# Attention 0: the rotation's cosine product of heads 1 to 7, from the matmul's bank on VectorE instead of from ScalarE's copy on GpSimd

## The chip, the cores and the metric

The kernel runs on one core of a Trainium2 chip. The metric is the device time of one execution in microseconds, and a kernel's time is the median of its runs. A core's engines work side by side and each takes its instructions in order: TensorE (PE in the profile, its weight loads PEld), VectorE (DVE), ScalarE (ACT), GpSimd (POOL) and SyncE (SP), whose queue issues the DMAs. Matmul results land in banks of PSUM, which VectorE and ScalarE read; GpSimd works on SBUF.

## What is computed

Two layers over 1024 tokens of width 1024, float32. Layer 0 is differential attention, and the change lies in it:

```python
q = _rope(q.reshape(b, s, 2 * DA_HEADS, DA_QK_DIM), positions)
k = _rope(k.reshape(b, s, 2 * DA_HEADS, DA_QK_DIM), positions)
...
sc = jnp.einsum('bqhcd,bkhcd->bhcqk', qb, k, preferred_element_type=f32) * scale
p = jax.nn.softmax(sc, axis=-1)
p = p[:, :, 0] - lam * p[:, :, 1]
return jnp.einsum('bhqk,bkhd->bqhd', p.astype(v.dtype), v)
```

with 8 heads of two 64-wide parts each, and the rotation

```python
x1, x2 = xf[..., :half], xf[..., half:]
out = jnp.concatenate([x1 * cos - x2 * sin, x2 * cos + x1 * sin], axis=-1)
```

A normalization over each head's output, a SiLU gate and an output projection follow; layer 1 is latent attention (MLA), which has a rotation of its own that the change does not touch.

## The kernel before

Matmul operands are split into a high and a low part in float32r, and each product is three matmuls (L173 to L175). Projections are made transposed: a strip of 128 weight columns against 512 tokens (a half) gives a bank of 128 x 512 (`acc`); a head of layer 0 has a k, a q and a z strip of two halves each. Attention 0 goes head by head. For each tile of 128 queries (`q_tile`) TensorE makes two scores of 128 x 1024 (`s`, L866), VectorE takes the negated maximum (`nm`, L412), ScalarE the exponential (L414, `e`, and in place in `s`), VectorE combines the two (L872 to L874, `e`). TensorE transposes that in two halves (`tr`, L395), ScalarE copies the high part (`pth`, L397), VectorE subtracts the low part (`ptl`, L398), and TensorE multiplies by the values (`pv`). Between these pieces TensorE makes the strips of the next head, some steps at a time (`stream0`, the table `FILL0`): so the rotation of head 1's strips runs from 157 us on, and that of head 7's to about 628 us.

When a half of a k or q strip is done, `rope` takes its bank: ScalarE copies it to SBUF (`rp_raw`, L331, or L333 with the scale for q), four DMAs on SP's queue swap its blocks of 32 partitions into `rp_sw` (L335), and `rp_r` gets the product with the cosines (L336). Some steps of the stream later, GpSimd makes the product of the swapped tile with the sines (L341) and the sum (L343). Then ScalarE and GpSimd split the result for the scores: for k in `stack_k` (L356 to L359, `ks`), for q in `stack_q` (ScalarE L364 and L365, `qa`; GpSimd L366 and L367, `qb`; then four DMAs on SP's queue, L369 and L370). In heads 1 to 7 the product and the sum are GpSimd's; in head 0 VectorE makes both. 7 heads x k and q x 2 halves make 28 rotations.

GpSimd also makes the low parts of the weights (`wl`, L219), the gate (`o`, L938), the scaling by the head's norm (L908), products for the output projection (`ob`, L1112 to L1123) and the power in the norm (`rq_y`, L169). The norm's sums come from eight matmuls (`ssq`, L945) that use a bank of the same rotation as the strips, and VectorE turns them into `sl_w` and `sl_f` (L949 to L951) for GpSimd's L169.

The order of each engine's instructions is made by the framework's scheduler from the program's order and its own costs; `in_turn` keeps an instruction in the program's order on its engine (nearly all of GpSimd's), `behind` puts one behind a mark of the softmax. Buffers are rings by tag: all of `rope`'s tiles come from one of six. Two banks serve `acc` in turn.

Of the kernel before, what the change touches and what calls it, by code (L numbers as in the profile page):

```python
# [16 lines left out]
ALU = mybir.AluOpType  # L17
# [55 lines left out]
SC0 = 64 ** -0.5  # L73
# [8 lines left out]
def trunk(ctx: ExitStack, tc: tile.TileContext, A, out):  # L82
    nc = tc.nc
    SP, PE, V, S, G = nc.sync, nc.tensor, nc.vector, nc.scalar, nc.gpsimd

    def pool(stack, name, bufs=1, side="left", space=None):
        kw = dict(name=name, bufs=bufs, reuse_waits="tile")
        if space is not None:
            kw["space"] = space
            if space == DRAM:  # L90
                kw.pop("reuse_waits")
        else:
            kw["side"] = side
        return stack.enter_context(tc.tile_pool(**kw))
# [21 lines left out]
    def bank(tag, name, shape=None):  # L116
        nonlocal turn
        if tag == "acc":
            turn += 1
            if (turn - 1) % (2 + NB.get("accx", 0)) < 2:  # L120
                return psa.tile([P, HF], F32, name=name, tag="acc", bufs=2)
            tag = "accx"
        return ps.tile(shape or [P, HF], F32, name=name, tag=tag, bufs=NB[tag])
# [20 lines left out]
    cosT = const.tile([P, T], F32, name="cosT")  # L144
# [35 lines left out]
    def behind(eng):  # L180

        return tc.issue_after(mk[eng]) if eng in mk else nullcontext()

    def in_turn(ins):

        return tc.keep_in_program_order(ins) if mk else ins
# [134 lines left out]
                self.count += 1  # L321
                side.tick()

    def rope(rp, acc, half, scale, eng=G, add=V):

        cs = slice(half * HF, half * HF + HF)
        raw = rp.tile([P, HF], F32, name="rp_raw", tag="rp", bufs=6)
        sw = rp.tile([P, HF], F32, name="rp_sw", tag="rp", bufs=6)
        r = rp.tile([P, HF], F32, name="rp_r", tag="rp", bufs=6)
        if scale == 1.0:  # L330
            S.copy(raw, acc)  # L331
        else:
            S.mul(raw, acc, scale)  # L333
        for q in range(4):
            SP.dma_start(sw[q * 32 : q * 32 + 32], raw[(q ^ 1) * 32 : (q ^ 1) * 32 + 32])  # L335
        r_ = eng.tensor_mul(r, raw, cosT[:, cs])  # L336
        if eng is G:
            in_turn(r_)

        def rot():  # L340
            in_turn(G.tensor_mul(sw, sw, sinT[:, cs]))  # L341
            if add is G:
                in_turn(G.tensor_add(r, r, sw))  # L343

        def fin():
            if add is not G:
                with behind("V"):
                    V.tensor_add(r, r, sw)
            return r

        return rot, fin

    def stack_k(t, r):

        with behind("S"):
            S.copy(t[0:64, 0, :], r[0:64])  # L356
            S.copy(t[64:128, 1, :], r[64:128])
        in_turn(G.tensor_sub(t[64:128, 0, :], r[0:64], f32v(t[0:64, 0, :])))
        in_turn(G.tensor_sub(t[0:64, 1, :], r[64:128], f32v(t[64:128, 1, :])))  # L359

    def stack_q(qa, qb, r):

        with behind("S"):
            S.copy(qa[0:64, 0, :], r[0:64])  # L364
            S.copy(qa[64:128, 1, :], r[64:128])  # L365
        in_turn(G.tensor_sub(qb[0:64, 0, :], r[0:64], f32v(qa[0:64, 0, :])))  # L366
        in_turn(G.tensor_sub(qb[64:128, 1, :], r[64:128], f32v(qa[64:128, 1, :])))  # L367
        for t in (qa, qb):
            SP.dma_start(f32v(t[64:128, 0, :]), f32v(t[0:64, 0, :]))  # L369
            SP.dma_start(f32v(t[0:64, 1, :]), f32v(t[64:128, 1, :]))  # L370
# [133 lines left out]
    wp = pool(stW, "wp0", side="right")  # L504
# [262 lines left out]

    def k_done(h):
        def f(acc, half):
            rot, fin = rope(wp, acc, half, 1.0, *[G if h else V] * 2)  # L770

            def g():
                t = a0a.tile([P, 2, HF], F32R, name="ks", tag="ks", bufs=4)
                stack_k(t, r.pop() if r else fin())
                KS.setdefault(h, [None, None])[half] = t

            r = []
            sum_ = [lambda: r.append(fin()), None] if h else []
            side.add(*[None] * ROT, rot, *[None] * (DEF - 1 - ROT), *sum_, g)
        return f  # L780

    def q_done(h):
        def f(acc, half):
            rot, fin = rope(wp, acc, half, SC0, *[G if h else V] * 2)

            def g():
                qa = a0a.tile([P, 2, HF], F32R, name="qa", tag="qs", bufs=4)
                qb = a0a.tile([P, 2, HF], F32R, name="qb", tag="qs", bufs=4)
                stack_q(qa, qb, r.pop() if r else fin())
                QS.setdefault(h, [None, None])[half] = qa, qb  # L790

            r = []
            sum_ = [lambda: r.append(fin()), None] if 0 < h < 5 else []
            side.add(*[None] * ROT, rot, *[None] * (DEF - 1 - ROT - (h == NH - 1)), *sum_, g)
        return f
# [728 lines left out]
    for n, rows, acc, f in ((3, 4, Z, 1), (4, 0, Z, 1), (5, 4, Y, 1), (6, 4, Y, 0)):  # L1524
# [5 lines left out]
        for i in range(4):  # L1530
# [24 lines left out]
            if i == 1 and n == 5:  # L1555
                raws = [[], []]
                with tc.issue_after(w6):
                    for k, (tag, nb) in enumerate((("wraw", 2), ("gz", 3))):
                        for f in range(2):
                            raw = wst.tile([P, HF], F32, name="wraw", tag=tag, bufs=nb)  # L1560
# [27 lines left out]
    wp = pool(stw, "wp1", side="right")  # L1588
# [432 lines left out]
    def qp_done(h):  # L2021
        def f(acc, half):
            rot, fin = rope(wp, acc, half, SC1, G, G if h or half else V)

            def g():
                qa = ap.tile([P, 2, HF], F32R, name="qpa", tag="qps", bufs=4)
                qb = ap.tile([P, 2, HF], F32R, name="qpb", tag="qps", bufs=4)
                stack_q(qa, qb, fin())
                QP.setdefault(h, [None, None])[half] = qa, qb

            side.add(None, rot, *[None] * (h > 0 and not half))
            if h and half:
                late_q.append(g)
            elif half:
                first_q.append(g)
            else:
                side.add(g)
        return f
# [209 lines left out]
    def add_to(tt, acc, f, a=0, b=HF, piece=False):  # L2248
        full = xs_[tt]
        cs = slice(f * HF + a, f * HF + b)  # L2250
        add = V.tensor_add(full[:, cs], full[:, cs], acc[:, a:b])
        if not piece:
            return add.ins
        early = tt // 4
        ss = sm.tile([P, 1], F32, name="tss")
        junk = p6.tile([P, HF], BF16, name="tjunk", tag="tjunk", bufs=1)
        sq = S.activation(junk[:, : b - a], full[:, cs], AF.Square, accum_out=ss).ins
        final = f != early and b == HF
        w = w_[tt] if early else w4[:, tt : tt + 1]
        if f == early:  # L2260
            V.tensor_scalar(w, ss, 1.0 / D, EPS, op0=ALU.mult, op1=ALU.add)
            G.tensor_mul(full[:, cs], full[:, cs], fg[:, cs])
        else:
            sums = V.scalar_tensor_tensor(out=w, in0=ss, scalar=1.0 / D, in1=w, op0=ALU.mult, op1=ALU.add).ins
        if not final:
            return add.ins
        if tt == NT - 1:
            for f_, ins in zip(held, (sums, sq)):
                with tc.issue_after(ins):
                    f_()  # L2270
        if early:
            scale(tt, rsqrt(w, 1)[:, 0:1])
        elif tt == 3:
            y4.append(rsqrt(w4, 4))
# [72 lines left out]
    for n, first, rows, acc, f, piece in ((3, True, 4, Z, 1, False), (4, False, 0, Z, 1, True), (5, False, 4, Y, 1, True)):  # L2347
        sp = sv.splits(n + 1)
        for i in range(4):
# [5 lines left out]
            add = add_to(rows + i, acc[i], f, piece=piece)  # L2355
# [8 lines left out]
    for tiles, a, b in LAST1:  # L2364
        acc = {i: bank("z", "oyb") if a else Y[i] for i in tiles}
# [87 lines left out]
```

## Time and profile before

| | before |
|---|---|
| median of 3 runs, us | 1395.75 (1395.17 to 1396.02) |
| profiled execution, us | 1394.95 |
| its span, us | 1393.2 |
| granted TensorE clock | 0.999 |
| busy us: PE, PEld | 1367.5, 1144.7 |
| busy us: DVE, ACT, POOL | 928.3, 740.9, 753.1 |

The profile is of one execution, and its times are from the span's start. A group's row gives the line, engine, operation, the tile written and those read, count, busy time and mean. A timeline's row gives start, duration, engine, line, operation and tiles, and in square brackets the engine's idle time ahead of it with what ended it. Matmuls are pipelined, so that rows of TensorE overlap. "x36" for L336 in the page counts the eight rotations of layer 1 that are GpSimd's as well.

### The profile page before, as it was taken

To read this page: it belongs to the slowest core of one execution; us is meant where nothing else is said; L and a number is where in the kernel's file an instruction comes from. 1 tells how busy PE (TensorE), PEld (TensorE's weight loads), DVE (VectorE), ACT (ScalarE), POOL (GpSimd) and SP (SyncE) were. 2 spreads that over 40 slices of the span, in tenths; PEclk is the share of its full clock that TensorE was granted. 3 is DMA by queue.
4 is the path that set the end of the run, shared out by engine and by line. 5 is a ranking of instruction groups with operands and counts; after the bars stand their busy time and mean duration, and the time that the engine had idled before them with its cause. 6 is when DMAs were issued, how large, how long until landed. Compare 5 with 4: busy or idle time off the path is not lost.

```text
span 1393.2 us, 20695 instructions
## 1 busy us (share of the span) xinstructions
PE 1367.5 (98%) x7334; PEld 1144.7 (82%) x7334; DVE 928.3 (67%) x1313; ACT 740.9 (53%) x1339; POOL 753.1 (54%) x593
## 2 busy tenths in 40 slices
PE   9999999999999999999999999999999999999997
PEld 6788888888888887887887888888888888888886
DVE  7655777777666666668596976545656555555684
ACT  5532465656565555567648553335454544545554
POOL 5424374758686858575794233532141373834673
PEclk9999999999999999999999999999999999999999
DMA  9857644343444434526564246489443364667463
GB/s 342 263 177 244 201 110 141 100 144 105 149 127 144 128 121 122 151 61 212 182 219 167 68 137 212 137 282 286 125 105 119 102 201 136 193 221 215 145 245 121
DMA packets 149386, 232.06 MB, mean 167 GB/s; under 512 B 20641, under 2 KB 57633, under 8 KB 149282
## 3 DMA queue, kind: packets, MB, share of 16 engines
q1 hardware_dynamic: 149282, 230.74, 52.7%
q8 instruction: 58, 0.95, 0.3%
q14 instruction: 46, 0.38, 0.1%
HBM read 144.74 MB, written 61.81 MB: 148 GB/s over the span
## 4 chain that ended last, share of the span: by engine, by line
PE 79%; DVE 6%; DMA 5%; ACT 3%; POOL 3%; issue 2%; SPq 1%; POOLq 0%; ACTq 0%; DVEq 0%
PE s L2067 10%; PE acc L173 9%; PE acc L175 9%; PE acc L174 9%; PE tr L395 7%; PE s L866 7%; PE pv L173 4%; PE pv L174 4%; PE pv L175 4%; PE vps L173 2%; PE vps L174 1%; PE vps L175 1%; PE zacc L175 1%; PE zacc L173 1%; PE zacc L174 1%
## 5 line engine op out<-in xcount | busy, mean ns | idle before, releaser
L397 ACT CAST pth<-tr 128x512 fp32r<-128x512 f32 x256 | 150.3, 587 | 285.7 <-PE tr L395 280.8
L412 DVE TENSOR_REDUCE nm<-s 128x1 f32<-128x1024 f32 x192 | 233.8, 1218 | 79.8 <-PE s L866 70.9
L398 DVE TENSOR_TENSOR ptl<-tr,pth 128x512 fp32r<-128x512 f32 x256 | 176.1, 688 | 150.3 <-ACT pth L397 146.3
L219 POOL TENSOR_TENSOR wl<-wraw,wh 128x512 fp32r<-128x512 f32 (+2 forms) x77 | 98.8, 1284 | 208.4 <-ACT wh L218 176.3
L414 ACT ACTIVATE e<-s,nm 128x1024 f32<-128x1024 f32 x128 | 143.5, 1121 | 35.4 <-DVE nm L412 35.0
L395 PE MATMUL tr<-ident,e 128*128 128x128 f32 x1024 | 155.0, 273 | 4.1 <-DVE ptl L398 3.8
L395 PEld LDWEIGHTS tr<-ident,e 128*128 128x128 f32 x1024 | 120.7, 140 | 46.5 <-DVE ptl L398 24.1
L173 PE MATMUL acc<-h0h,wh 128*128 128x512 f32 x360 | 150.2, 417 | 0.0
L173 PE MATMUL pv<-pth,vt 128*128 128x256 f32 x512 | 147.5, 288 | 0.0
L174 PE MATMUL pv<-ptl,vt 128*128 128x256 f32 x512 | 145.6, 284 | 0.0
L175 PE MATMUL pv<-pth,vt 128*128 128x256 f32 x512 | 144.6, 282 | 0.0
L175 PE MATMUL acc<-h0h,wl 128*128 128x512 f32 x360 | 141.5, 393 | 0.0
L174 PE MATMUL acc<-h0l,wh 128*128 128x512 f32 x360 | 141.1, 392 | 0.0
L336 POOL TENSOR_TENSOR rp_r<-rp_raw,cosT 128x512 f32<-128x512 f32 x36 | 47.0, 1305 | 104.4 <-ACT rp_raw L333 52.9
L173 PEld LDWEIGHTS pv<-pth,vt 128*128 128x128 f32 x512 | 97.2, 190 | 2.9 <-ACT pth L397 0.2
L174 PEld LDWEIGHTS pv<-ptl,vt 128*128 128x128 f32 x512 | 97.4, 190 | 2.4
L175 PEld LDWEIGHTS pv<-pth,vt 128*128 128x128 f32 x512 | 97.3, 190 | 0.0
L1199 POOL TENSOR_TENSOR wol<-wol,woh 128x512 fp32r<-128x512 f32 x56 | 82.3, 1492 | 26.0 <-ACT woh L1198 24.4
L866 PE MATMUL s<-ks,qa 128*128 128x512 f32 x256 | 82.7, 403 | 4.4 <-DVE e L874 3.2
L874 DVE SCALAR_TENSOR_TENSOR e<-s,z,e 128x1024 f32<-128x1024 f32 x64 | 82.2, 1284 | 2.2
L866 PE MATMUL s<-ks,qb 128*128 128x512 f32 x256 | 79.8, 393 | 1.2 <-DMA qb<-qb 1.2
L175 PEld LDWEIGHTS acc<-h0h,wl 128*128 128x128 f32 x360 | 67.6, 188 | 15.1
(427 smaller groups left out, 3461.1 us busy)
## 6 DMA issues: line engine op xcount, KB each, us to landing
ada<-in_ada_ss SPq DMA_DIRECT2D x32, 512.0 KB, 5.9
wraw<-in_w_s SPq DMA_DIRECT2D x64, 256.0 KB, 2.8
vS<-v_hl SPq DMA_DIRECT2D x32, 512.0 KB, 5.9
vt<-vS SPq DMA_DIRECT2D x32, 512.0 KB, 4.9
wol<-tS SPq DMA_DIRECT2D x56, 256.0 KB, 5.2
tS<-ob SPq DMA_DIRECT2D x48, 256.0 KB, 2.0
rp_sw<-rp_raw SPq DMA_DIRECT2D x160, 64.0 KB, 2.0
bc_s<-bc_d SPq DMA_DIRECT2D x34, 256.0 KB, 4.2
```

The source lines that it names most:

```text
L173: PE.matmul(psum, ah, bh, start=first, stop=False, skip_group_check=skip)
L174: PE.matmul(psum, ah, bl, start=False, stop=False, skip_group_check=skip)
L175: mm3.last = PE.matmul(psum, al, bh, start=False, stop=last, skip_group_check=skip).ins
L219: sub = (V if pair_of else G).tensor_sub(l_[:, :n], raw[:, :n], f32v(h_[:, :n]))
L395: transpose_p.last = PE.transpose(tr[:, j, :], p[:, kt * P : (kt + 1) * P], ident).ins
L397: mk["S"] = S.copy(pth[kh][:, :, dst], tr).ins
L398: mk["V"] = V.tensor_sub(ptl[kh][:, :, dst], tr, f32v(pth[kh][:, :, dst])).ins
L412: mk["V"] = V.reduce_max(nm, s_ps, axis=AX.X, negate=True).ins
L414: mk["S"] = S.activation(e, s_ps, AF.Exp, bias=nm, scale=1.0, accum_out=zs).ins
L866: PE.matmul(s_ps[:, kc * HF : (kc + 1) * HF], src[:, c, ql], KS[h][kc][:, c, :], start=fst, stop=not fst)
L1199: sub = eng.tensor_sub(lo, raw, f32v(hi))
L2067: PE.matmul(s_ps[:, kc * HF : (kc + 1) * HF], lhs, rhs(kc), start=i == 0, stop=i == 4)
```

## The change

`rope` gets a flag, which `k_done` and `q_done` set for heads 1 to 7. With it, VectorE multiplies the bank by the scale and the cosines in one instruction; GpSimd's product of ScalarE's copy is gone from those rotations. The copy and the swap stay.

```diff
-    def rope(rp, acc, half, scale, eng=G, add=V):
+    def rope(rp, acc, half, scale, eng=G, add=V, bank_=False):
...
         for q in range(4):
             SP.dma_start(sw[q * 32 : q * 32 + 32], raw[(q ^ 1) * 32 : (q ^ 1) * 32 + 32])
-        r_ = eng.tensor_mul(r, raw, cosT[:, cs])
-        if eng is G:
-            in_turn(r_)
+        if bank_:
+            V.scalar_tensor_tensor(out=r, in0=acc, scalar=scale, in1=cosT[:, cs], op0=ALU.mult, op1=ALU.mult)
+        else:
+            r_ = eng.tensor_mul(r, raw, cosT[:, cs])
+            if eng is G:
+                in_turn(r_)
...
-            rot, fin = rope(wp, acc, half, 1.0, *[G if h else V] * 2)
+            rot, fin = rope(wp, acc, half, 1.0, *[G if h else V] * 2, h > 0)
...
-            rot, fin = rope(wp, acc, half, SC0, *[G if h else V] * 2)
+            rot, fin = rope(wp, acc, half, SC0, *[G if h else V] * 2, h > 0)
```

The new product is line 337; the lines after it stand three further down in the changed kernel (L398 is L401 there). VectorE is not held to the program's order, so the scheduler places the 28 products. On VectorE at the q strip of head 1 (some 180 us into the span before; `rp_r` is the rotated tile, `z` the softmax's sums, `ada` a product of the modulation), before:

```order
L412 TENSOR_REDUCE nm<-s 128x1 [waits PE_49]
L398 TENSOR_TENSOR ptl<-tr,pth 128x4x128 [waits Activation_49]
L436 ISA ada,modb_105<-ada,c_202,vec 128x1024 [waits DMAHW1_49]
L436 ISA modb_105 128x1
L872 RECIPROCAL z_1670<-z_1670 128x1 [waits Activation_49]
L873 TENSOR_SCALAR z_1670<-z_1670,zz,neglam 128x1 [waits DVE_49]
L874 SCALAR_TENSOR_TENSOR e<-s,z_1670,e 128x1024 [waits DVE_49]
```

and in the changed kernel:

```order
L415 TENSOR_REDUCE nm<-s 128x1 [waits PE_49]
L401 TENSOR_TENSOR ptl<-tr,pth 128x4x128 [waits Activation_49]
L439 ISA ada,modb_105<-ada,c_202,vec 128x1024 [waits DMAHW1_49]
L439 ISA modb_105 128x1
L875 RECIPROCAL z_1670<-z_1670 128x1 [waits Activation_49]
L337 SCALAR_TENSOR_TENSOR rp_r<-acc,cosT 128x512 [waits Activation_49,Pool_49]
L876 TENSOR_SCALAR z_1670<-z_1670,zz,neglam 128x1 [waits DVE_49]
L877 SCALAR_TENSOR_TENSOR e<-s,z_1670,e 128x1024 [waits DVE_49]
```

One instruction came in; it waits for ScalarE, whose copy reads the same bank, and for GpSimd's last use of the buffer that `rp_r` takes over. On GpSimd at the k and q strips of head 5 (460 to 474 us), before:

```order
L1119 TENSOR_TENSOR ot_4671<-ob_4305,ob_4304 128x512 [waits Pool_49]
L336 TENSOR_TENSOR rp_r<-rp_raw,cosT 128x512 [waits Activation_49]
L358 TENSOR_TENSOR ks<-rp_r,ks 64x512 [waits Activation_49,Pool_49]
L359 TENSOR_TENSOR ks<-rp_r,ks 64x512 [waits Activation_49]
L219 TENSOR_TENSOR wl<-wraw,wh 128x512 [waits PE_49,Activation_49,Pool_49]
L938 TENSOR_TENSOR o<-o,gz 128x512 [waits Activation_49]
L1122 TENSOR_TENSOR ob_4304<-ot_4671,ob_4304 128x512
L1123 TENSOR_TENSOR ob_4305<-ob_4305,ot_4671 128x512 [waits DMAHW1_49]
L341 TENSOR_TENSOR rp_sw<-rp_sw,sinT 128x512 [waits DMAHW3_49,DMAHW4_49,DMAHW2_49,DMAHW1_49]
L343 TENSOR_TENSOR rp_r<-rp_r,rp_sw 128x512 [waits Pool_49]
```

and in the changed kernel:

```order
L1122 TENSOR_TENSOR ot_4671<-ob_4305,ob_4304 128x512 [waits Pool_49]
L361 TENSOR_TENSOR ks<-rp_r,ks 64x512 [waits Activation_49,Pool_49]
L362 TENSOR_TENSOR ks<-rp_r,ks 64x512 [waits Activation_49]
L219 TENSOR_TENSOR wl<-wraw,wh 128x512 [waits PE_49,Activation_49,Pool_49]
L941 TENSOR_TENSOR o<-o,gz 128x512 [waits Activation_49]
L1125 TENSOR_TENSOR ob_4304<-ot_4671,ob_4304 128x512
L1126 TENSOR_TENSOR ob_4305<-ob_4305,ot_4671 128x512 [waits DMAHW1_49]
L344 TENSOR_TENSOR rp_sw<-rp_sw,sinT 128x512 [waits DMAHW3_49,DMAHW4_49,DMAHW2_49,DMAHW1_49]
L346 TENSOR_TENSOR rp_r<-rp_r,rp_sw 128x512 [waits DVE_49,Pool_49]
```

The product is gone, the rest stands in the same order, and the sum waits for VectorE. On TensorE at the q strip's neighbourhood of head 4 (365 us), where the sums of the norm are made, before:

```order
L866 MATMUL s<-ks,qb 128x512 x2
L945 MATMUL ssq<-ones,osq 128x1 [waits Activation_49]
L945 MATMUL ssq<-ones,osq 128x1 x3
L173 MATMUL acc<-h0h_1_120,wh 128x512
L174 MATMUL acc<-h0l_1_121,wh 128x512
L175 MATMUL acc<-h0h_1_120,wl 128x512
L395 MATMUL tr<-ident,e 128x128 [waits DVE_49]
```

and in the changed kernel:

```order
L398 MATMUL tr<-ident,e 128x128 [waits DVE_49]
L398 MATMUL tr<-ident,e 128x128 x3
L173 MATMUL acc<-h0h_1_124,wh 128x512
L174 MATMUL acc<-h0l_1_125,wh 128x512
L175 MATMUL acc<-h0h_1_124,wl 128x512
L869 MATMUL s<-ks,qa 128x512 [waits DVE_49]
L948 MATMUL ssq<-ones,osq 128x1 [waits DVE_49]
L948 MATMUL ssq<-ones,osq 128x1 x3
L869 MATMUL s<-ks,qa 128x512
```

Those matmuls moved behind the next transposes and into the next tile's score, and wait for VectorE's product where they waited for ScalarE. They moved so in two heads; in five earlier ones they stay in place and wait for VectorE too. In some tiles TensorE's transposes stand a step of the stream later or earlier than before; the instructions are the same.

## The prediction

> **What bounds the kernel now.** I read the page's busy times and chain first, then busy time by stretch of the span, then TensorE's own waits in order of time, and last what GpSimd, ScalarE and VectorE do ahead of each of those waits.
>
> ```profile
> PE 1367.5 (98%) x7334; PEld 1144.7 (82%) x7334; DVE 928.3 (67%) x1313; ACT 740.9 (53%) x1339; POOL 753.1 (54%) x593
> PE 79%; DVE 6%; DMA 5%; ACT 3%; POOL 3%; issue 2%; SPq 1%; POOLq 0%; ACTq 0%; DVEq 0%
> ```
>
> TensorE is busy for 1367.5 of 1393.2 us and makes 79% of the chain that ended last. No change to VectorE or GpSimd is worth more than the TensorE waits that they cause, so the question is which of these lie where the products are.
>
> ```profile
> 157.00:330.00 173.00, 172.91 (x972) 147.81 (x971) 133.59 (x191) 105.41 (x187) 113.51 (x89) 1.00 0.42 120
> 330.00:400.00 70.00, 69.41 (x389) 58.53 (x387) 49.23 (x70) 41.25 (x74) 50.82 (x43) 1.00 0.44 132
> 400.00:470.00 70.00, 68.54 (x387) 58.16 (x387) 46.85 (x66) 40.34 (x71) 54.92 (x46) 1.00 0.44 136
> 470.00:540.00 70.00, 68.29 (x380) 56.82 (x378) 46.75 (x65) 40.45 (x72) 51.11 (x43) 1.00 0.45 138
> 540.00:640.00 100.00, 98.31 (x553) 82.80 (x552) 69.82 (x99) 59.19 (x104) 67.61 (x56) 1.00 0.39 115
> 640.00:700.00 60.00, 56.12 (x322) 46.31 (x321) 41.59 (x66) 38.49 (x73) 38.98 (x33) 1.00 0.65 211
> ```
>
> The columns are the stretch, its length, then busy time of PE, PEld, DVE, ACT and POOL, TensorE's clock, DMA share and GB/s. From 157 to 640 us, where the 28 products lie, TensorE idles for 0.09 + 0.59 + 1.46 + 1.71 + 1.69 = 5.5 us. GpSimd is busy for 338 of these 483 us (70%), VectorE for 346 (72%). After 640 no product runs. These are TensorE's waits there:
>
> ```profile
> 334.49 0.73 PE L866 MATMUL s<-ks,qa 128*128 128x512 f32 x2 [0.59 <-DVE e L874]
> 409.96 0.70 PE L866 MATMUL s<-ks,qa 128*128 128x512 f32 x2 [0.88 <-DMA qa<-qa]
> 411.22 0.70 PE L866 MATMUL s<-ks,qb 128*128 128x512 f32 x2 [0.55 <-DMA qb<-qb]
> 475.10 0.66 PE L395 MATMUL tr<-ident,e 128*128 128x128 f32 x4 [0.87 <-DVE ptl L398]
> 490.83 0.73 PE L866 MATMUL s<-ks,qa 128*128 128x512 f32 x2 [0.65 <-DVE e L874]
> 543.54 0.73 PE L866 MATMUL s<-ks,qa 128*128 128x512 f32 x2 [0.32 <-DVE e L874]
> 551.32 0.70 PE L866 MATMUL s<-ks,qb 128*128 128x512 f32 x2 [0.66 <-DMA qb<-qb]
> 561.02 0.74 PE L866 MATMUL s<-ks,qa 128*128 128x512 f32 x2 [0.30 <-DVE e L874]
> 615.16 0.66 PE L395 MATMUL tr<-ident,e 128*128 128x128 f32 x4 [0.40 <-DVE ptl L398]
> ```
>
> Nine waits, 5.22 us together. That is all the change can win in this stage. It can lose more, because most of these waits end on VectorE, which gets the work.
>
> **What is removed and added.** The tile of the products, and VectorE's nearest row, a product of a bank and an SBUF tile with the same shape:
>
> ```profile
> L336 POOL TENSOR_TENSOR rp_r<-rp_raw,cosT x28: 1264/1294/1392, 158.1 to 617.7; 128x512 f32<-128x512 f32 x28
> L802 DVE SCALAR_TENSOR_TENSOR gz<-zth,acc x20: 665/684/689, 110.9 to 860.5; 128x512 f32<-128x512 f32 x20
> ```
>
> GpSimd loses 28 x 1.294 = 36.2 us, VectorE gains 28 x 0.684 = 19.2 us. ScalarE's copy of the bank stays, since the four swap DMAs read it; no DMA is added or taken away. Neither sum is a time by itself.
>
> **Where GpSimd's 1.3 us reaches TensorE.** Ahead of the wait at 475.10:
>
> ```profile
> 460.18 1.30 POOL L336 TENSOR_TENSOR rp_r<-rp_raw,cosT 128x512 f32<-128x512 f32 x1
> 470.64 1.29 POOL L343 TENSOR_TENSOR rp_r<-rp_r,rp_sw 128x512 f32<-128x512 f32 x1
> 471.96 0.62 ACT L364 CAST qa<-rp_r 64x512 fp32r<-64x512 f32 x1 [2.23 <-POOL rp_r L343]
> 473.74 0.58 ACT L397 CAST pth<-tr 128x512 fp32r<-128x512 f32 x1
> 474.36 0.69 DVE L398 TENSOR_TENSOR ptl<-tr,pth 128x512 fp32r<-128x512 f32 x1 [0.94 <-ACT pth L397]
> ACT qa L364 <- POOL rp_r L343: 9.5, 6, 2.3
> ```
>
> GpSimd works without a gap from 460 to 472, so the sum L343 is late; ScalarE stands still for 2.23 us behind it, with the next softmax's copy queued after it; VectorE's subtraction follows, and TensorE waits 0.87. Without the product at 460.18 all of this comes 1.3 us earlier, more than 0.87: I take the whole wait. The wait at 490.83 has the same form one half later (the last row: ScalarE waits for L343 9.5 us in all, six times, 2.3 at most), because SP issues that half's swap DMAs behind the qb transfer that GpSimd releases: 0.65, taken whole too. At 334.49 it goes through VectorE itself:
>
> ```profile
> 331.63 1.28 POOL L336 TENSOR_TENSOR rp_r<-rp_raw,cosT 128x512 f32<-128x512 f32 x1
> 331.72 1.22 DVE L951 TENSOR_SCALAR sl_w<-sl_w 128x4 f32<-128x4 f32 x1
> 333.15 1.28 DVE L874 SCALAR_TENSOR_TENSOR e<-s,z,e 128x1024 f32<-128x1024 f32 x1
> L951 DVE TENSOR_SCALAR sl_w<-sl_w x16: 152/170/1221, 196.4 to 689.1; 128x4 f32<-128x4 f32 x16
> ```
>
> A 128x4 instruction with a median of 170 ns takes 1.22 us here and ends when the GpSimd product ends: it stood behind it. The next GpSimd instruction needs its result, so without the product nothing is in its way: 1.05 us earlier against a wait of 0.59, taken whole. At 410:
>
> ```profile
> 404.53 1.28 POOL L336 TENSOR_TENSOR rp_r<-rp_raw,cosT 128x512 f32<-128x512 f32 x1
> 407.14 1.29 POOL L367 TENSOR_TENSOR qb<-rp_r,qa 64x512 fp32r<-64x512 f32 x1
> 409.49 0.52 SPq L370 DMA_DIRECT2D qb<-qb  x1
> ```
>
> GpSimd has two products in the backlog ahead of L367, but SP's queue issues in order and follows by only one of them, 1.3 us. That takes the 0.88 and some 0.2 of the 0.55: 1.1. Of the three waits at 543 to 561 (0.32 + 0.66 + 0.30 = 1.28), which hang on one more late L951 and on a qb transfer, I take half, 0.6, since their swap transfer and the head's output on ScalarE end close by. The one at 615 I leave. Sum: 0.87 + 0.65 + 0.59 + 1.1 + 0.6 = **3.8 us**; ends 0 (every chain has something else just behind) and 5.2 (all nine).
>
> **What VectorE's 0.68 us costs.** In the new order each product waits for ScalarE's copy of the same bank, so it can't start earlier than the GpSimd one did; the built order has it at 28 places. Laying 0.69 us into VectorE's timeline at each, after its predecessor there or the copy, whichever ends last, delays the next VectorE instruction by 11.0 us in all; the rest falls where VectorE stood idle. TensorE pays only where its own instruction stands closer behind. The first and the last of seven such places:
>
> ```profile
> 157.51 1.21 DVE L412 TENSOR_REDUCE nm<-s 128x1 f32<-128x1024 f32 x1
> 159.07 0.69 DVE L398 TENSOR_TENSOR ptl<-tr,pth 128x512 fp32r<-128x512 f32 x1 [0.35 <-ACT pth L397]
> 159.88 0.49 PE L395 MATMUL tr<-ident,e 128*128 128x128 f32 x3
> ...
> 507.80 1.22 DVE L412 TENSOR_REDUCE nm<-s 128x1 f32<-128x1024 f32 x1
> 508.93 0.68 DVE L398 TENSOR_TENSOR ptl<-tr,pth 128x512 fp32r<-128x512 f32 x1
> 510.07 0.38 PE L395 MATMUL tr<-ident,e 128*128 128x128 f32 x2
> ```
>
> At 159 the product fills the idle 0.35 and delays the subtraction by 0.34; the transposes come 0.12 after it, so TensorE loses 0.22. At 509 there is no idle time: 0.77 against a margin of 0.46, a loss of 0.31. The five between read 0.47, 0.47, 0.11, 0.40 and 0.20. Sum **2.2 us**; ends 0 (TensorE's order also moved at such places, transposes later) and 11.0 (no margin anywhere).
>
> The waits it adds: seven of the ssq matmuls, which reuse the bank just finished, now wait for VectorE's product instead of ScalarE's copy. In the timeline the product would end 0.4 us or more ahead of each, and two of them moved 2 to 3 us later in TensorE's order, so I cost this at nothing; the cover is gone if VectorE is over 0.4 us later there. Behind a product that waits, VectorE holds the next softmax's maximum.
>
> Net 2.2 - 3.8 = -1.6 us. The profiled execution took 1394.95 us and goes to about 1393.35; the median of the three runs stands 0.8 above it, so I predict 1395.75 - 1.6 = **1394.1**.
>
> **A rule of the notes.** The Trainium skill, Perfetto Trace Analysis, Optimizing Scalar/DVE Operations, says that GpSimd and VectorE share an SBUF read port, so that moving work between them might not help; SBUF — State Buffer, Who interferes with whom, limits this to VectorE instructions with two SBUF inputs or in a two-port mode. The L951 row agrees with the sharing and the L802 row with the limit; by the first page alone the time would be that of the third rival below.
>
> **Rivals.** *The backlog unwinds.* GpSimd's lateness is a queue, and 11% less work (36 of 338 us) may drain it wholly: all nine waits go, 5.2, and VectorE's cost falls to about 1 with the L951 stretches gone: -4.2, 1391.5. For it: five of the nine have GpSimd in their chain. Against: the margins of TensorE elsewhere are as thin.
>
> *VectorE is held by ScalarE* (slower). Product waits for copy, copy for L364, L364 for GpSimd; now VectorE stands in that line too, with the softmax's maximum behind it. It decides once the copies land more than about 1 us later than in this trace, which uses up the idle time at the places read above: then all of the 11.0 is paid, less the 3.8 won: +7.2, 1403.0. Against: in the timeline the copy has ended when VectorE gets to the product, or ends in idle time there, and GpSimd's relief makes the copies earlier.
>
> *The products contend.* If each stood behind a running GpSimd instruction as L951 did, half of 1.29 us in 70% of cases, 28 x 0.645 x 0.70 = 12.6 us more of VectorE, a fifth of it (2.2 / 11.0) paid by TensorE: +2.5, net +0.9, 1396.7. Against: the spread of L802, 665 to 689 ns, beside a GpSimd that is as busy.
>
> **How the numbers follow.** 0.2% of 1395.75 is 2.8 us, about what a measurement here can tell from no change: faster is below 1392.95, slower above 1398.55. The forecast and the contention, both inside, hold 0.50 (the contention 0.08 of it); the unwound backlog 0.33; VectorE held, and anything like it above 1398.55, 0.17. The range runs from 1390.5, all nine waits gone at no cost (5.2 below), to 1399.5, half of the way to the held VectorE, which leaves about 0.1 on each side.
>
> **What would show it.** Right: 28 products on VectorE at 0.67 to 0.69 us; GpSimd down by 36 us; ScalarE's waits for L343's sum well under 9.5 us; no TensorE wait near 334, 475 and 490; new waits of 0.2 to 0.5 us on the subtraction or the combination in heads 1 to 3. Wrong: products of over 0.8 us, ssq matmuls waiting for VectorE, or TensorE's idle time from 157 to 640 above 5.5 us. The prediction fails most easily if the waits that vanish come back at other tiles.

## The result and the profile after

Three comparisons of the changed kernel with the kernel before were made, each with its own runs of both:

| comparison | before, median us | changed, median us (lowest to highest) | ratio, 95% interval | that is |
|---|---|---|---|---|
| with the prediction | 1396.02 | 1392.52 (1390.75 to 1394.0) | 0.9973 [0.9962, 0.9985] | -3.8 us [-5.3, -2.1] |
| repeated (e5) | 1395.86 | 1394.17 (1391.49 to 1397.15) | 0.9986 [0.9978, 0.9995] | -2.0 us [-3.1, -0.7] |
| repeated (e11) | 1396.21 | 1394.26 (1391.55 to 1395.95) | 0.9985 [0.9976, 0.9994] | -2.1 us [-3.4, -0.8] |

The changed kernel is faster by 2 to 4 us, some 0.2%; the mean of the three is 2.6. The forecast was 1.6, the first rival (the backlog unwinds) 4.2. The first comparison's interval holds the rival's time and leaves out the forecast; in both repeats it is the other way round.

From the page of the changed kernel and its busy time by stretch, columns as before:

```profile
PE 1367.2 (98%) x7334; PEld 1145.0 (82%) x7334; DVE 942.0 (68%) x1341; ACT 741.5 (53%) x1339; POOL 717.9 (52%) x565
```

```profile
157.00:330.00 173.00, 172.42 (x970) 147.54 (x969) 141.67 (x202) 104.52 (x185) 98.61 (x77) 1.00 0.42 122
330.00:400.00 70.00, 70.00 (x394) 59.72 (x393) 49.98 (x74) 42.58 (x76) 47.71 (x40) 1.00 0.44 132
400.00:470.00 70.00, 69.25 (x390) 58.53 (x389) 48.02 (x71) 40.21 (x72) 51.08 (x43) 1.00 0.47 141
470.00:540.00 70.00, 69.13 (x383) 57.65 (x383) 49.22 (x72) 40.77 (x72) 46.26 (x39) 1.00 0.44 138
540.00:640.00 100.00, 99.30 (x563) 83.97 (x563) 73.69 (x110) 60.20 (x106) 60.41 (x51) 1.00 0.39 114
```

GpSimd lost 35.2 us over the span, of 36.2 worked out. VectorE gained 16.3 us in these stretches (346.3 to 362.6), not 19.2. Rows of VectorE that follow one another without a gap overlap by 0.08 us (the product at 507.50 takes 0.68, and the next row starts at 508.10, as shown further down), so that a product between two others adds only 0.60 us of busy time: 28 x 0.60 = 16.8, an estimate. TensorE now idles from 157 to 640 us for 0.58 + 0.00 + 0.75 + 0.87 + 0.70 = 2.9 us, where it was 5.5. These are its waits of over 0.1 us there:

```profile
166.79 0.73 PE L869 MATMUL s<-ks,qa 128*128 128x512 f32 x2 [0.58 <-DVE e L877]
409.40 0.70 PE L869 MATMUL s<-ks,qa 128*128 128x512 f32 x2 [0.19 <-DMA qa<-qa]
410.63 0.70 PE L869 MATMUL s<-ks,qb 128*128 128x512 f32 x2 [0.53 <-DMA qb<-qb]
489.37 0.73 PE L869 MATMUL s<-ks,qa 128*128 128x512 f32 x2 [0.73 <-DVE e L877]
549.33 0.70 PE L869 MATMUL s<-ks,qb 128*128 128x512 f32 x2 [0.43 <-DMA qb<-qb]
558.98 0.73 PE L869 MATMUL s<-ks,qa 128*128 128x512 f32 x2 [0.27 <-DVE e L877]
```

Of the nine waits of before those at 334, 475, 543 and 615 are gone, that at 410 is smaller, those at 411, 490, 551 and 561 are still there, and one at 166.8 is new. The products themselves, and ScalarE's wait for GpSimd's sum, which was 9.5 us in all:

```profile
L337 DVE SCALAR_TENSOR_TENSOR rp_r<-acc,cosT x28: 670/686/693, 159.3 to 614.5; 128x512 f32<-128x512 f32 x28
...
ACT qa L367 <- POOL rp_r L346: 5.5, 6, 1.7
```

**How the profiled execution adds up.** It took 1393.23 us, 1.7 below that of before. VectorE's row maximum `nm` is a good clock inside a trace: its first and its 121st instruction bracket the 28 products. Of before and of after:

```profile
141.84 1.21 DVE L412 TENSOR_REDUCE nm<-s 128x1 f32<-128x1024 f32 x1
...
649.40 1.21 DVE L412 TENSOR_REDUCE nm<-s 128x1 f32<-128x1024 f32 x1
```

```profile
142.53 1.22 DVE L415 TENSOR_REDUCE nm<-s 128x1 f32<-128x1024 f32 x1
...
646.83 1.22 DVE L415 TENSOR_REDUCE nm<-s 128x1 f32<-128x1024 f32 x1
```

The stage shrank from 507.6 to 504.3 us, 3.3 less. The first maximum came 0.7 us later (141.84, 142.53) and the part after the stage took 0.8 us longer; I put neither down to the change: its instructions lie in between, in the three profiles of the changed kernel the first maximum lies anywhere from 142.5 to 144.1, and the part after the stage takes 743.4 to 745.7 us in the thirteen profiles here, with the same lines of the kernel. (It is 744.6 in all three of the changed kernel and 743.8 in the only one of before, so a small effect there is not excluded.) So below I give the stage's length and TensorE's idle time from 157 to 640 us beside each timed ratio: the ratio says whether a kernel is faster, the two others say where.

### The profile page after: what moved, and what is told of

It is laid out like the page before. It is cut to its first block, busy times and chain, and to the rows that moved or that the text cites. A ratio compares the mean times of both kernels' runs of the same rounds, so it can differ in the third digit from the quotient of the medians.

```text
span 1391.4 us, 20739 instructions
## 1 busy us (share of the span) xinstructions
PE 1367.2 (98%) x7334; PEld 1145.0 (82%) x7334; DVE 942.0 (68%) x1341; ACT 741.5 (53%) x1339; POOL 717.9 (52%) x565
## 4 chain that ended last, share of the span: by engine, by line
PE 81%; DVE 6%; DMA 5%; ACT 3%; issue 2%; POOL 2%; SPq 1%; POOLq 0%; DVEq 0%; ACTq 0%
PE s L2070 10%; PE acc L175 9%; PE acc L173 9%; PE acc L174 9%; PE s L869 8%; PE tr L398 8%; PE pv L173 4%; PE pv L175 4%; PE pv L174 4%; DMA ada<-in_ada_ss 2%; PE oy L174 1%; PE oy L175 1%; PE oy L173 1%; PE zacc L173 1%; PE zacc L174 1%
## 5 line engine op out<-in xcount | busy, mean ns | idle before, releaser
L401 DVE TENSOR_TENSOR ptl<-tr,pth 128x512 fp32r<-128x512 f32 x256 | 176.1, 688 | 144.3 <-ACT pth L400 139.6
L219 POOL TENSOR_TENSOR wl<-wraw,wh 128x512 fp32r<-128x512 f32 (+2 forms) x77 | 99.3, 1291 | 260.8 <-ACT wh L218 186.9
L417 ACT ACTIVATE e<-s,nm 128x1024 f32<-128x1024 f32 x128 | 143.5, 1121 | 39.7 <-DVE nm L415 39.5
L398 PE MATMUL tr<-ident,e 128*128 128x128 f32 x1024 | 155.0, 273 | 3.4 <-DVE ptl L401 3.1
L398 PEld LDWEIGHTS tr<-ident,e 128*128 128x128 f32 x1024 | 120.8, 140 | 45.0 <-DVE ptl L401 22.9
L174 PEld LDWEIGHTS acc<-h0l,wh 128*128 128x128 f32 x360 | 68.2, 189 | 9.2
```

The lines of the kernel that those rows point to most:

```text
L174: PE.matmul(psum, ah, bl, start=False, stop=False, skip_group_check=skip)
L219: sub = (V if pair_of else G).tensor_sub(l_[:, :n], raw[:, :n], f32v(h_[:, :n]))
L398: transpose_p.last = PE.transpose(tr[:, j, :], p[:, kt * P : (kt + 1) * P], ident).ins
L401: mk["V"] = V.tensor_sub(ptl[kh][:, :, dst], tr, f32v(pth[kh][:, :, dst])).ins
L417: mk["S"] = S.activation(e, s_ps, AF.Exp, bias=nm, scale=1.0, accum_out=zs).ins
```

## Experiments

| kernel | median us, beside before | ratio, 95% interval | stage, us | TensorE idle 157 to 640, us |
|---|---|---|---|---|
| before | | | 507.6 | 5.5 |
| changed, three profiles | see above | | 504.3, 505.1, 503.9 | 2.9, 3.1, 2.7 |
| e1 relief alone | 1392.42, 1396.19 | 0.9976 [0.9967, 0.9986] | 505.7 | 3.3 |
| e2 VectorE's cost alone | 1398.96, 1396.19 | 1.0021 [1.0013, 1.003] | 510.0 | 6.8 |
| e3 heads 4 to 7 | 1394.22, 1396.19 | 0.9984 [0.9976, 0.9993] | 505.0 | 2.8 |
| e4 heads 1 to 3 | 1397.32, 1396.19 | 1.0004 [0.9996, 1.0013] | 509.0 | 5.0 |
| e6, e10 all but the first product | 1392.54, 1395.86; 1392.12, 1396.21 | 0.9977 [0.9968, 0.9986]; 0.9967 [0.9955, 0.998] | 504.1, 502.9 | 2.8, 1.7 |
| e7 from ScalarE's copy | 1395.95, 1395.86 | 1.0001 [0.9993, 1.001] | 506.2 | 3.7 |
| e8 qb transfers after the swaps | 1393.34, 1395.86 | 0.9978 [0.9969, 0.9987] | 507.5 | 4.1 |
| e9 two swaps on ScalarE's queue | 1393.0, 1396.21 | 0.9972 [0.9961, 0.9983] | 505.0 | 3.4 |

The profiled executions of e1, e8 and e9 were the slowest of their runs (6.0, 2.6 and 1.1 us above the median), so their stage may read high. What the stage and what the median say of a kernel agree to some 1.6 us, e8 aside.

### Relief and cost apart (e1, e2)

e1 leaves the product out, so that GpSimd is relieved and VectorE gets nothing:

```diff
         if bank_:
-            V.scalar_tensor_tensor(out=r, in0=acc, scalar=scale, in1=cosT[:, cs], op0=ALU.mult, op1=ALU.mult)
+            pass
...
-                in_turn(G.tensor_add(r, r, sw))
+                in_turn(G.tensor_add(r, raw if bank_ else r, sw))
```

> Left out: the cosine product itself (the sum takes ScalarE's copy instead of the product), for heads 1 to 7. So GpSimd loses 28 x 1.29 us and VectorE gets nothing: the relief alone. As predicted (relief 3.8 us, VectorE's products 2.2 us): before less 3.8, which is 1392.2, and 1 to 2 us faster than the changed kernel less its measured net. Rival, VectorE's products cost nothing but the one new wait of 0.58 us at 167: the same as the changed kernel within 0.6 us, 1391.9 to 1392.5, with that wait gone. Backlog rival: all nine waits gone, 1390.8. The wait near 490 (0.65) should stay, by the trace after, since no product stands ahead of it on GpSimd.

e2 has both products, VectorE's into a tile that nobody reads:

```diff
         if bank_:
-            V.scalar_tensor_tensor(out=r, in0=acc, ...)
-        else:
-            r_ = eng.tensor_mul(r, raw, cosT[:, cs])
+            V.scalar_tensor_tensor(out=rp.tile([P, HF], mybir.dt.bfloat16, name="rp_x", tag="rpx", bufs=1), in0=acc, ...)
+        if True:
+            r_ = eng.tensor_mul(r, raw, cosT[:, cs])
```

> GpSimd keeps its 28 products as before, and VectorE makes each a second time from the bank into a scratch tile that nobody reads (bf16, for room): VectorE's cost alone. As predicted: 2.2 us slower, 1398.2, with new TensorE waits of 0.1 to 0.5 us at seven places between 157 and 510. Rival, the built order puts the transposes later where a product stands ahead of a subtraction: at most one new wait of about 0.6, 1396.0 to 1396.6. VectorE held by ScalarE: 7 to 11 us slower, 1403 or more. GpSimd's nine waits stay in all three.

Relief alone: -3.4 us [-4.6, -2.0], the predicted 3.8 within the interval. Cost alone: +2.9 us [1.8, 4.2], the predicted 2.2 within it. That e2 came near the forecast is luck: its new waits stand near 167 and 407, none at the seven places of the prediction. If the two added up, the changed kernel would be 0.4 us faster; it is 2 to 4 us faster. With GpSimd relieved, VectorE's products cost little (0.8 us by the medians, 3.4 of e1 against 2.6, and nothing by TensorE's idle time, 3.3 against 2.9); with GpSimd as before, they cost about 3. The intervals alone would leave room for chance, but the traces show a mechanism at one place. In before, after and e2, the rows on the head output's way through ssq, the broadcast factor `bc_s` and GpSimd, up to the weight split that TensorE needs:

```profile
365.44 1.05 PE L945 MATMUL ssq<-ones,osq 128*128 128x1 f32 x8
376.25 1.55 POOL L908 TENSOR_TENSOR o<-o,bc_s 128x512 f32<-128x512 f32 x1 [1.83 <-DMA bc_s<-bc_d]
403.27 1.29 POOL L219 TENSOR_TENSOR wl<-wraw,wh 128x512 fp32r<-128x512 f32 x1
```

```profile
367.05 0.68 DVE L337 SCALAR_TENSOR_TENSOR rp_r<-acc,cosT 128x512 f32<-128x512 f32 x1
367.78 1.05 PE L948 MATMUL ssq<-ones,osq 128*128 128x1 f32 x8
380.11 1.55 POOL L911 TENSOR_TENSOR o<-o,bc_s 128x512 f32<-128x512 f32 x1 [3.88 <-DMA bc_s<-bc_d]
402.70 1.29 POOL L219 TENSOR_TENSOR wl<-wraw,wh 128x512 fp32r<-128x512 f32 x1
```

```profile
368.28 0.68 DVE L337 SCALAR_TENSOR_TENSOR rp_x<-acc,cosT 128x512 bf16<-128x512 f32 x1
369.01 1.05 PE L948 MATMUL ssq<-ones,osq 128*128 128x1 f32 x8
381.08 1.54 POOL L911 TENSOR_TENSOR o<-o,bc_s 128x512 f32<-128x512 f32 x1 [3.63 <-DMA bc_s<-bc_d]
406.16 1.26 POOL L219 TENSOR_TENSOR wl<-wraw,wh 128x512 fp32r<-128x512 f32 x1
407.47 0.50 PE L175 MATMUL acc<-h0h,wl 128*128 128x512 f32 x1 [1.30 <-DVE nm L415]
```

By their maxima near 343 the changed kernel stands 0.4 us and e2 1.6 us behind before here. In both ssq now follows the product, some 2 us later, and GpSimd gets the factor 3.2 to 3.5 us later and stands still for it (3.88 and 3.63 instead of 1.83). The changed kernel has the 1.3 us products out of GpSimd's queue, and at 403 its weight split is even 0.6 us ahead of before (1.0 with the 0.4 that it stood behind). In e2 they are still in the queue, in which GpSimd works without a gap from 381 to the split; the split is 2.9 us behind before (1.3 without the 1.6), and TensorE waits 1.30: the profile names VectorE's maximum, which ends at the same time, but the operand is `wl`, and L219 ends at 407.42 (the row of the weight load there names `wl`). This is the larger of e2's two new waits of over half a microsecond; the other is the 0.58 near 167. With smaller ones won and lost TensorE's idle time grew by 1.2 us; the rest of the 2.9 is not placed.

The backlog rival expected all nine waits gone in e1. They aren't: 0.53 at 414, 0.66 at 493, 1.63 at 554 (0.66 in before) and 0.19 at 563 stand there, without any cost of VectorE's. That rival's time came near, its mechanism did not.

### Heads 4 to 7, and heads 1 to 3 (e3, e4)

The flag is `h > 3` in e3, and `0 < h < 4` in e4, instead of `h > 0`.

> Only the products of heads 4 to 7 (after about 343 us) on VectorE, heads 1 to 3 as before. If the gain lies where GpSimd has a backlog, nearly all of it is here: the waits at 410, 475, 543 and 615 go or shrink (0.85 + 0.9 + 0.6 + 0.5 = 2.9 us by the two traces), the one at 334 (0.6) stays, no wait at 167: about 2.9 less, 1393.1. If it were spread evenly over the 28 products it would be 16/28 of 3.3 = 1.9, 1394.1.

> Only the products of heads 1 to 3 (157 to about 343 us) on VectorE, heads 4 to 7 as before. By the two traces: the wait at 334 (0.6 to 0.9) goes, one of 0.58 comes at 167, the waits from 410 on stay: 0.3 less, 1395.7, no change that can be measured. Spread evenly over the products: 12/28 of 3.3 = 1.4 less, 1394.6.

e3 gave -2.2 us [-3.4, -1.0], e4 +0.6 [-0.6, 1.8]. A gain spread evenly over the products would be -1.9 for e3 and -1.4 for e4: e3's interval holds that as well as the -2.9 expected, but it lies outside e4's. So the gain is in heads 4 to 7, where GpSimd has its backlog. Row by row it went as the two traces had said, but for the wait near 551, which e4 should have kept and has not. e3 keeps the wait at 334 (0.55 at 336); e4 keeps those at 410 and 475:

```profile
411.34 0.70 PE L869 MATMUL s<-ks,qa 128*128 128x512 f32 x2 [1.21 <-DMA qa<-qa]
...
477.94 0.66 PE L398 MATMUL tr<-ident,e 128*128 128x128 f32 x4 [0.89 <-DVE ptl L401]
```

e4's stage holds a dip of the granted clock to 0.98 between 400 and 470 us, so its 509.0 reads some 1.4 high (0.02 x 70, an estimate).

### The first product (e5, e6, e10, e11)

The one new wait, at 166.8, is not at any of the seven places of the prediction. VectorE's modulation sum (L436 before, L439 after) and GpSimd's sine product there, in before, in after and in e10:

```profile
161.78 1.27 DVE L436 CUSTOM_DVE_ANT_0 ada<-ada,c,vec 128x1024 f32<-128x1024 f32 x1
161.97 2.23 POOL L341 TENSOR_TENSOR rp_sw<-rp_sw,sinT 128x512 f32<-128x512 f32 x1 [1.04 <-DMA rp_sw<-rp_raw]
```

```profile
162.65 1.29 POOL L344 TENSOR_TENSOR rp_sw<-rp_sw,sinT 128x512 f32<-128x512 f32 x1 [0.99 <-DMA rp_sw<-rp_raw]
162.87 2.15 DVE L439 CUSTOM_DVE_ANT_0 ada<-ada,c,vec 128x1024 f32<-128x1024 f32 x1
```

```profile
163.65 1.28 DVE L439 CUSTOM_DVE_ANT_0 ada<-ada,c,vec 128x1024 f32<-128x1024 f32 x1
163.83 2.25 POOL L344 TENSOR_TENSOR rp_sw<-rp_sw,sinT 128x512 f32<-128x512 f32 x1 [1.03 <-DMA rp_sw<-rp_raw]
```

Whichever starts first takes 1.3 us, and the other takes nearly its own time plus what is left of the first (2.23 of 2.37 us in before, 2.15 of 2.34 in after). In before VectorE is 0.19 us ahead and GpSimd, which has time, pays. The product at 159.3 pushes VectorE back by some 0.4 us against GpSimd, now it is 0.22 us behind, and it pays 0.88: e, the maximum and TensorE's scores follow. To test it, e6 and e10 leave that one product on GpSimd (`h > 1 or h == 1 and half == 1` for k), which takes one row from VectorE's order and puts one into GpSimd's.

> 27 of the 28 products on VectorE; the first (head 1, k, half 0, at 159 us) stays on GpSimd. Theory: that one product delays VectorE's L439 by 0.2 us past the start of GpSimd's L344, so that L439 waits 0.9 us for it instead of the other way round. Then here L439 starts 0.2 us ahead of L344 and takes 1.27 us, L344 takes 2.2, no wait near 167, 0.6 us less than the changed kernel: 1391.9. Rival, L439 is long for another reason (its own transfer, the weight split): wait near 167 stays, time as the changed kernel.

> The kernel with the first product on GpSimd again, beside the changed kernel on the same chip: L439 near 163 at 1.27 us and L344 at 2.2 us, no wait near 167; 0.6 to 1.3 us less than the changed kernel (the stage was 0.2 and 1.0 us shorter than in the two profiles of that one). Rival: equal within 0.3 us, the 0.58 won there being lost again by 640.

> The changed kernel beside it: L439 near 163 at 2.15 us, the wait of 0.58 near 167; 2 to 4 us below before, as in the two comparisons so far (2.0 and 3.8).

> The changed kernel once more, for what repeats from one profile to the next. If the waits come from the order and the durations, not from chance: the same five or six TensorE waits in 157 to 640 us within 0.15 us each, the modulation sum L439 near 163 again 2.15 us long behind GpSimd's L344, the wait of 0.58 near 167 again; time 3.5 us below before, 1392.5.

L439 takes 1.28 us again in both, the wait is gone, and the median is 1.6 and 2.1 us below that of the changed kernel on the same chip (1392.54 beside 1394.17, 1392.12 beside 1394.26), where 0.6 and 0.6 to 1.3 were expected. The intervals of the two kernels overlap in each comparison, so the size is not settled; that it beats both kernels agrees in both comparisons, and in the stage (503.5 us in the mean of two, 504.4 of three). From the first to the 25th maximum alone it is 98.3 us in both e6 and e10, 98.1 before, and 99.0, 99.6 and 99.0 in the three profiles of the changed kernel. The flip repeats: in the five profiles of kernels with that product on VectorE from the bank (after, e2, e4, e5, e11) the sum takes 2.13 to 2.15 us, in the five that have it on GpSimd, or nowhere (before, e1, e3, e6, e10), 1.27 or 1.28 us; e7 (2.14) and e8 and e9 (1.28), which come below, fit as well.

The Trainium skill, SBUF — State Buffer, Who interferes with whom, says that the order of issue decides which of the two engines blocks, and, of VectorE's two-port modes, that the first one holds the shared pair for its whole instruction. The rows agree: 0.2 us of lead decide over 0.9 us, to either side. Whether this sum runs in such a mode no run here shows.

e5 expected the time of the first comparison, 3.5 us below before; it came 2.0 below. e5 and e11 also show what repeats of the other waits: those near 411 (0.53 to 0.55) and 490 (0.73 or 0.74) in all three profiles; that near 550 ranges over 0.43, 0.82 and none, and depends on when a transfer lands.

### From the copy instead of from the bank (e7)

```diff
-            rot, fin = rope(wp, acc, half, 1.0, *[G if h else V] * 2, h > 0)
+            rot, fin = rope(wp, acc, half, 1.0, V, G if h else V)
```

> All 28 products on VectorE, but from ScalarE's copy in SBUF (two SBUF inputs) and not from the bank. If two SBUF inputs make VectorE wait for a running GpSimd instruction: products from 0.69 up to about 1.9 us, mean near 1.3, some GpSimd instructions over 2 us, and by the prediction's sum for contention 2.5 us over the changed kernel, 1395. If the port plays no part, 0.69 us throughout and the changed kernel's time, 1392.5.

The groups of VectorE's products from 157 to 640 us, busy time and mean ns behind the bar, of e7 and of the changed kernel:

```profile
L339 DVE TENSOR_TENSOR rp_r<-rp_raw,cosT 128x512 f32<-128x512 f32 x28 | 26.0, 930 | 7.0 <-ACT rp_raw L331 3.2 <-ACT rp_raw L333 1.4 <-POOL ob L1125 0.9
```

```profile
L337 DVE SCALAR_TENSOR_TENSOR rp_r<-acc,cosT 128x512 f32<-128x512 f32 x28 | 19.2, 685 | 5.8 <-ACT rp_raw L331 3.2 <-ACT rp_raw L333 1.2 <-POOL ob L1115 0.8
```

The same product on the same engine takes 930 ns in the mean from SBUF and 685 from the bank. The mean hides two kinds: eighteen of e7's products take 0.67 to 0.69 us, and ten, each started while a GpSimd instruction ran, take 1.02 to 1.80. By the medians the time is that of before: the whole gain is gone, 1.8 us beside e5 and more beside the first comparison. The trace shows less of it: TensorE idles 3.7 us where the changed kernel idles 2.7 to 3.1 and before 5.5, and the rest of the 1.8 is not placed. So the third rival's mechanism is real, at half its size (6.8 us more of VectorE, not 12.6; the 2.5 that it charges to TensorE is near what the medians say), and it is the bank as a source that keeps it away from this change. Of the two pages of the Trainium skill weighed in the prediction, the trace agrees with the limit of the second (an instruction with one SBUF input isn't slowed: 670 to 693 ns, all 28); the first one's warning against moving work between these engines holds for e7 and not for the change.

### The wait near 490 (e8, e9)

The prediction took this wait as gone (0.65); it is 0.73. In the changed kernel the rows ahead of it are:

```profile
475.54 0.68 DVE L337 SCALAR_TENSOR_TENSOR rp_r<-acc,cosT 128x512 f32<-128x512 f32 x1
476.18 2.45 SPq L335 DMA_DIRECT2D rp_sw<-rp_raw  x4
480.24 1.29 POOL L344 TENSOR_TENSOR rp_sw<-rp_sw,sinT 128x512 f32<-128x512 f32 x1 [4.64 <-DMA rp_sw<-rp_raw]
481.61 1.29 POOL L346 TENSOR_TENSOR rp_r<-rp_r,rp_sw 128x512 f32<-128x512 f32 x1
482.99 1.22 DVE L415 TENSOR_REDUCE nm<-s 128x1 f32<-128x1024 f32 x1 [1.01 <-PE s L869]
483.58 0.62 ACT L368 CAST qa<-rp_r 64x512 fp32r<-64x512 f32 x1
484.22 1.11 ACT L417 ACTIVATE e<-s,nm 128x1024 f32<-128x1024 f32 x1
```

The product is not late, and GpSimd stands still ahead of the sine product and the sum, behind which ScalarE waits 1.67 for its first copy to qa. The swaps leave 4 us after ScalarE's copy (which ended at 472.07): they stand behind the transfers of qa and qb in SyncE's queue, and the last of these waits for GpSimd's qb product. In before:

```profile
475.73 1.29 POOL L367 TENSOR_TENSOR qb<-rp_r,qa 64x512 fp32r<-64x512 f32 x1
477.10 1.29 POOL L336 TENSOR_TENSOR rp_r<-rp_raw,cosT 128x512 f32<-128x512 f32 x1
```

The moved product of this half stood behind qb on GpSimd and had kept nothing. The one at 460.18, which the prediction shows, did stand ahead of it. Without it the second qb product, the swaps and the sum come 1.4 us sooner (475.73 to 474.31, 477.60 to 476.18, 483.06 to 481.61; 0.5 of that had been won before 460). But TensorE comes 1.5 us sooner as well (490.83 to 489.37), since the wait at 475 is gone: the prediction counted one product of 1.3 us for two waits that follow one another, 0.87 + 0.65. And by the last three rows a sooner sum alone could not have won this wait. The maximum, which hangs on TensorE's scores, and the second copy to qa end together, at 484.21 and 484.20 (485.63 and 485.65 in before, within 0.06 us in the nine other profiles with this order), and the exponential (L417) comes behind both: it needs the maximum, and it stands behind the copy on ScalarE.

e8 issues the qb transfers of the first half behind the swaps, in heads 5 and 6, on top of e6 (its lines from 330 on read 6 to 10 higher):

```diff
+            last = SP.dma_start(sw[q * 32 : q * 32 + 32], raw[(q ^ 1) * 32 : (q ^ 1) * 32 + 32]).ins
+        flush_qb(last)
...
+            if late and t is qb:
+                qb_late.extend(d)
+            else:
+                [f() for f in d]
```

> The kernel with the first product on GpSimd, and in heads 5 and 6 the two qb transfers of the first half are issued behind the second half's swap transfers instead of ahead of them. Theory: the waits near 490 (0.73) and 549 (0.5) come from SyncE's queue, where the swaps stand 4 us behind transfers that wait for GpSimd's qb; here the swaps go out right after ScalarE's copy, ScalarE's wait for the sum near 481 goes, and both TensorE waits with it: 1.2 us less than with the first product alone, 1390.7. Rival, GpSimd's own backlog makes that sum late: the waits stay.

```profile
475.78 2.45 SPq L341 DMA_DIRECT2D rp_sw<-rp_raw  x4
482.02 0.70 PE L879 MATMUL s<-ks,qb 128*128 128x512 f32 x2 [0.98 <-DMA qb<-qb]
```

The swaps still stood behind the qa and weight transfers, but they left 1.9 us after ScalarE's copy (which ended at 473.85), where it had been 4.1. That brought little: GpSimd's sine product started 8.15 us after the copy began, instead of 8.77. And qb itself came late, a new wait of 0.98; the wait near 490 grew to 1.11. e9 takes these swaps out of SyncE's queue altogether: `(S if on_s else SP).dma_start(...)`, with `on_s` for the second half of q in heads 5 and 6.

> The kernel with the first product on GpSimd, and the second half's swap transfers of heads 5 and 6 (two of 28 products) issued on ScalarE's queue instead of SyncE's, so that they stand behind no transfer that waits for GpSimd. Theory: the waits near 490 (0.73) and 549 (0.5) come from SyncE's queue: the swaps leave 2 to 3 us earlier, GpSimd's sum and ScalarE's copy for qa follow, and both waits go, 1.2 us less than with the first product alone, if ScalarE's four issues of about 0.6 us each (SyncE's row) find idle time. Rival: ScalarE has no room there (its copies pth follow at once), and new waits of up to 2 us on the subtraction take their place.

```profile
471.12 4.16 ACTq L335 DMA_DIRECT2D rp_sw<-rp_raw  x4
479.36 1.28 POOL L344 TENSOR_TENSOR rp_sw<-rp_sw,sinT 128x512 f32<-128x512 f32 x1 [4.73 <-DMA rp_sw<-rp_raw]
484.69 0.66 PE L398 MATMUL tr<-ident,e 128*128 128x128 f32 x4 [1.17 <-DVE ptl L401]
```

The swaps now left right after ScalarE's copy, which had begun at 470.49, and the sine product still started 8.87 us after that, no sooner than in the changed kernel. So the order of SyncE's queue is hardly what keeps the swapped tile: the sooner its transfers were issued, the longer they took, from issue to landing 2.2 us in the median in the changed kernel, 4.0 in e8 and 4.3 in e9. The DMA engines are busy there (0.67 to 0.99 in stretches of 2 us from 470 to 478 us in e9); that they are the reason was not tested. The four issues also held ScalarE for 4.2 us, the scheduler put the copies for qa ahead of pth, and a wait of 1.17 stands at 485 where there was none. The one near 490 is gone, and that near 549 (0.75) stayed. With -3.9 us [-5.4, -2.4] e9 is no better than e6 and e10. What would win the wait near 490 stays open, since each of the two experiments moved another wait into its place.

## Why the prediction was right, and where its steps were off

The range and the direction held. That the forecast itself came within some 1 us of the mean (1.6 beside 2.6) is in part luck: it had both the relief and the cost too high, and the two errors partly cancel. By its own steps, with the nine waits as the measure:

- **GpSimd's relief, 3.8 forecast.** Gone or less: 0.87 at 475 (taken whole, right), 0.59 at 334 (right), 0.71 of 1.43 at 410 and 411 (1.1 forecast), 0.58 of 1.28 at 543 to 561 (0.6), 0 of 0.65 at 490 (taken whole: wrong), and 0.40 at 615, which had been left. Sum 3.15; e1's time says 3.4 [2.0, 4.6]. The step that failed is the one at 490: that SP issues that half's swaps behind the qb transfer is right, but the product taken out ahead of that transfer is the one already counted at 475, so that TensorE came sooner by as much, and VectorE's maximum ends with the copy that the sum releases.
- **VectorE's cost, 2.2 forecast at seven places.** None of the seven shows in the changed kernel; 0.58 shows at an eighth. This is the term that was mis-sized, and it makes the net 2.6 of TensorE's idle time instead of 1.6. The reason is the one named as its lower end: the built order moves TensorE's transposes. At the last of the seven places, after the change:

```profile
507.50 0.68 DVE L337 SCALAR_TENSOR_TENSOR rp_r<-acc,cosT 128x512 f32<-128x512 f32 x1
508.10 0.68 DVE L401 TENSOR_TENSOR ptl<-tr,pth 128x512 fp32r<-128x512 f32 x1
...
508.69 0.39 PE L173 MATMUL acc<-h0h,wh 128*128 128x512 f32 x1
508.92 0.39 PE L174 MATMUL acc<-h0l,wh 128*128 128x512 f32 x1
509.15 0.60 PE L398 MATMUL tr<-ident,e 128*128 128x128 f32 x4
```

  Two matmuls that stood behind the transposes now stand ahead of them, 0.46 us, and the subtraction ends at 508.8, 0.4 before TensorE asks for it. The price of a delay was read from the old order; the new order had been built with the delay in it.
- **The ssq matmuls, costed at nothing.** TensorE waits for none of them, but the cover was not the margin of 0.4 us: ssq itself moved some 2 us, and what hides that is GpSimd's relief. Without it (e2) this is where the largest new wait comes from.
- **VectorE held by ScalarE (+7.2).** Did not happen, not even in e2 with GpSimd unrelieved, where 7 to 11 us were expected of it and 2.9 came.
- **The products contend (+0.9).** Not here (670 to 693 ns, all 28), but in e7.
- **The backlog unwinds (-4.2).** Four of the nine waits went, not nine, and in e1 four stand without any cost of VectorE's; that the first comparison came near this time is luck.

## What to carry to other kernels

A busy queue is worth relieving where another engine stands behind its head: here 16 of the 28 products (heads 4 to 7) carried nearly all of the gain. Read the price of added work from the order that is built with it, since a scheduler may already have moved the consumer; and of a wait that you mean to remove, look for a second chain that ends at the same time, and count a removed instruction once for all the waits that follow it. Where two engines take turns, a delay of 0.4 us can pass a wait of 0.9 us to the engine that has no time.

## What was not expected of the hardware

A VectorE and a GpSimd instruction on SBUF took turns nearly whole: 1.27 and 2.23 us, or 2.15 and 1.29, by a lead of 0.2 us. A product of a bank and an SBUF tile was not touched by it (670 to 693 ns), the same product of two SBUF tiles took up to 1.8 us. Four transfers issued 4 us sooner landed no sooner: 4.3 us in the median from issue to landing, instead of 2.2. Their four issues took 2.45 us on SyncE's queue, and stretched over 4.2 and 5.0 us at the two places where they stood on ScalarE's, with both queues issuing.
